# RWKV scan on one Trainium2 core: its base solved for pairs of chunks, its second half prepared inside it, and modulation weights moved to VectorE beside the feed-forward

## The chip, the cores and the metric

The kernel runs on one core of one Trainium2 chip. The metric is device microseconds of one execution. Five engines work side by side, each through a queue of its own in order: TensorE (PE in the rows; PEld is its weight load), VectorE (DVE), ScalarE (ACT), GpSimd (POOL) and SyncE (SP), which issues most DMAs.

## The reference

Two models in a row, each of several layers at width 1024. The change lies in the first one, in layer 0. It works on 256 context tokens and 256 latent tokens; its mixer is RWKV on one half of the channels (8 heads of 64, forwards and backwards) and a Mamba block on the other, then comes a gated feed-forward. What the change touches:

```
m_lat = split(silu(c)     @ w_ada[i] + b_ada[i], 6)        # modulation, 6 x 1024 values for each of
m_ctx = split(silu(c_ctx) @ w_ada[i] + b_ada[i], 6)        # 2 layers and 2 conditions
...
logw  = rw_w0 + einsum('btdl,dlc->btdc', tanh(lw), rw_w_up)
decay = exp(-exp(-softplus(-logw) - 0.5))
iclr  = sigmoid(rw_a0 + einsum('btdl,dlc->btdc', la, rw_a_up))
kk    = k * rw_k_k / max(norm(k * rw_k_k), 1e-12)
k_dir = k * (1 + (iclr - 1) * rw_k_a)
def step(S, inp):                                          # one token, both directions, context then latent
    r_t, w_t, k_t, v_t, a_t, b_t = inp                     # a = -kk, b = kk * iclr
    sa = einsum('bhvk,bhk->bhv', S, a_t)
    S  = S * w_t + sa[..., None] * b_t + v_t[..., None] * k_t
    return S, einsum('bhvk,bhk->bhv', S, r_t)
...
h = h + m[2] * mixer(modulate(rms_norm(h), m[0], m[1]))
h = h + m[5] * ((silu(x @ w1) * (x @ w3)) @ w2)            # x = modulate(rms_norm(h), m[3], m[4])
```

## The kernel before

Activations lie with channels on partitions, 128 to a tile, and 512 tokens (T, two halves of S = 256) along the free axis. Weights come from DRAM as pieces `raw` through a ring of four buffers on SyncE's queue; ScalarE rounds a piece to `whi`, VectorE takes the rest `wlo` (`split`, L347 and L348), and TensorE multiplies high and low parts in three passes (L361, L362, L364).

**The modulation.** A chunk is 256 of the 6 x 1024 outputs of one layer: 1 MB of weights. `ada_steps` runs eight matmuls a chunk, in records of 128x256 (L396), ScalarE copies the sums (`adar`, L399), two small matmuls turn and fold them (L402) and VectorE adds the bias (`mod`, L405). `ada_rest` makes a generator of such chunks that other code advances. Of the 48 chunks 26 are made during the scan (layer 0, numbers 8 to 23, and layer 1, numbers 0 to 9), and 14 in the feed-forward of layer 0, one for each of its first slots.

**The preparation.** `rwkv_prep` makes, for all 512 tokens, the cumulated decay `cs`, the products `b` and the keys `kd` of both directions, four blocks of channels one after the other. It is done before the scan starts.

**The scan.** `rwkv` cuts each direction into 8 chunks of 64 tokens; step n takes chunk n of the forward direction and the matching one of the backward direction, 16 heads in all on two sets of partitions. For a step:

- `products`: exponentials `ew`, `ei` on ScalarE, the scaled tiles `ar` and `bkp` on VectorE and GpSimd (L734 to L741), the chunk's own products masked into `g` (L750, L751), and transposes `bt`.
- `base`: the 16x16 diagonal blocks of a triangular matrix are cut out of `g` (copies L768, then L770 and L771) and inverted by 15 rounds on VectorE: a shuffle gives a row of the block to all partitions of its group (`lb`, L777), a multiply (`lm`, L780) and an add into `s` (L782). The rounds shrink from 15 columns a head to 1.
- `inverse`: the blocks are set on a diagonal (`st`, L788) and joined to 64x64 by two levels of small matmuls (L793 to L805).
- `values` and `through`: the chunk's values `uv`, its outputs, and the update of the state `X` (add L848, decay by `wc` L849).

Base and products of a step are written ahead of the step that uses them: base two steps, products three. A scheduler lays the instructions of each engine in an order of its own; the loop only gives it their sequence. `fill` advances the modulation generator at places in `rwkv`; `bonus` (L898 to L904) and `rwkv_out` (L916 to L935) follow when their half of the tokens is done, and `mix_out` is the output projection behind it. The feed-forward (`gated`, `gate0`) then has slots of 48 matmuls of the first matrix, with `silu` and the product `gs`, `ghi`, `glo` behind each (L1178 to L1181), and slots of 32 matmuls of the second, with two adds into `x` behind each (L1226).

## Time and profile before

| | us |
|---|---|
| median of 3 runs (3050.88 to 3053.53) | 3051.7 |
| profiled execution | 3049.11 |
| its span | 3047.3 |
| TensorE busy | 2935.5 (96%) |
| VectorE busy | 2113.2 (69%) |
| ScalarE busy | 1592.5 (52%) |
| GpSimd busy | 774.2 (25%) |
| mean granted TensorE clock | 0.979 of full |

Busy is the time in which an engine has at least one instruction at work; the span runs from the first instruction to the last. A share is an average over stages with different limits, so stretches are read by themselves. In the rows `<-` stands between an output and its inputs; buffer numbers are left out. A group's mean mixes shapes where it says "+14 forms". A window's row begins with its bounds and its length, and ends with GB/s of all DMAs. In a time line the first number is the start, the second the duration; consecutive instructions of one kind are put together as x2, x3.

### The profile page before, as it was taken

Reading aid. Unit: us, or ns where it says so; the run is one execution under the profiler, and the core shown is the slowest. Engines: PE = TensorE matmul, PEld = TensorE weight load, DVE = VectorE, ACT = ScalarE, POOL = GpSimd, SP = SyncE. Lnnn points to the kernel's source line nnn. Section 1 sums busy time; section 2 is a strip of 40 time slices with the busy share of each in tenths; the row PEclk is TensorE's granted clock in tenths of the full one; section 3 lists DMA queues with packets and bytes.
Section 4 is the critical chain, followed back from the end, with each engine's and each line's share of the span. In section 5 each row is a group of like instructions: output and inputs, shape, how many; then the busy total and the mean of one; then the engine's idle time right before and its main releaser. Section 6 shows DMA issues by size and latency. Waiting matters only on the chain. (4 is left out here: it accounts for less than half of the span.)

```text
span 3047.3 us, 44960 instructions
## 1 busy us (share of the span) xinstructions
PE 2935.5 (96%) x17880; PEld 2453.4 (81%) x17880; DVE 2113.2 (69%) x2953; ACT 1592.5 (52%) x2007; POOL 774.2 (25%) x719
## 2 busy tenths in 40 slices
PE   7997899999999998999999999999999999999998
PEld 5884677887888777888888888878888888888887
DVE  5658987622223654998888898977697666669665
ACT  5644223432222555777777776755445545545553
POOL 0335442211022112000000000035264534434552
PEclk9998799999999999999999999999999999999999
DMA  6222234244423334999999999955533555553453
GB/s 229 70 66 70 84 111 148 104 166 146 137 75 114 110 97 154 346 359 331 363 345 337 357 350 362 340 176 186 197 132 120 192 175 199 170 195 107 150 176 128
DMA packets 132456, 584.75 MB, mean 192 GB/s; under 512 B 11792, under 2 KB 48912, under 8 KB 79760
## 3 DMA queue, kind: packets, MB, share of 16 engines
q1 hardware_dynamic: 126592, 575.35, 53.2%
q10 hardware_dynamic: 5648, 6.47, 0.9%
q8 instruction: 142, 2.33, 0.3%
q14 instruction: 74, 0.61, 0.1%
HBM read 580.73 MB, written 1.05 MB: 191 GB/s over the span
## 5 line engine op out<-in xcount | busy, mean ns | idle before, releaser
L348 DVE TENSOR_TENSOR wlo<-raw,whi 128x2048 fp32r<-128x2048 f32 (+2 forms) x497 | 1059.3, 2139 | 243.3 <-ACT whi L347 204.9
L347 ACT ACTIVATE whi<-raw 128x2048 fp32r<-128x2048 f32 (+2 forms) x500 | 886.5, 1784 | 418.8 <-PE bank L362 195.6
L372 PE MATMUL bank<-a,whi 128*128 128x512 f32 x1408 | 355.4, 395 | 5.1 <-DVE a L1693 5.1
L372 PEld LDWEIGHTS bank<-a,whi 128*128 128x128 f32 x1408 | 256.0, 190 | 51.7 <-DVE a L1693 5.4
L1361 PE MATMUL bank<-whi,xghi 128*128 128x512 f32 x704 | 282.3, 401 | 0.0
L1362 PE MATMUL bank<-whi,xglo 128*128 128x512 f32 x704 | 276.6, 393 | 0.0
L348 POOL TENSOR_TENSOR wlo<-raw,whi 128x2048 fp32r<-128x2048 f32 x3 | 13.9, 4646 | 790.2 <-ACT whi L347 790.2
L361 PE MATMUL bank<-cathi,whi 128*128 128x512 f32 (+1 forms) x608 | 212.6, 368 | 1.4 <-ACT x L1264 1.0
L362 PE MATMUL bank<-catlo,whi 128*128 128x512 f32 (+1 forms) x608 | 211.6, 364 | 1.5 <-DVE catlo L454 1.5
L375 PEld LDWEIGHTS bank<-a,wlo 128*128 128x128 f32 x1408 | 191.8, 190 | 13.6 <-DVE wlo L348 0.4
L375 PE MATMUL bank<-a,wlo 128*128 128x256 f32 x1408 | 196.5, 283 | 0.0
L1364 PE MATMUL bank<-wlo,xghi 128*128 128x512 f32 x704 | 192.2, 394 | 0.0
L1748 POOL TENSOR_TENSOR g<-gs,g 128x256 fp32r<-128x256 f32 x88 | 153.0, 1740 | 97.3 <-ACT g L1747 97.3
L372 PE MATMUL bank<-g,whi 128*128 128x512 f32 x704 | 171.2, 391 | 0.1
L1362 PEld LDWEIGHTS bank<-whi,xglo 128*128 128x128 f32 x704 | 132.4, 188 | 26.7
L1361 PEld LDWEIGHTS bank<-whi,xghi 128*128 128x128 f32 x704 | 132.2, 188 | 27.0
L1364 PEld LDWEIGHTS bank<-wlo,xghi 128*128 128x128 f32 x704 | 129.9, 188 | 29.6 <-DVE wlo L348 2.1
L372 PEld LDWEIGHTS bank<-g,whi 128*128 128x128 f32 x704 | 128.4, 188 | 24.4 <-POOL g L1748 0.3
L1613 PE MATMUL bank<-whi,gthi 128*128 128x512 f32 x352 | 139.7, 397 | 0.0
L361 PEld LDWEIGHTS bank<-cathi,whi 128*128 128x128 f32 x608 | 114.7, 190 | 29.3 <-issue 8.3
L1613 PE MATMUL bank<-whi,gtlo 128*128 128x512 f32 x352 | 138.1, 392 | 0.0
L364 PE MATMUL bank<-cathi,wlo 128*128 128x512 f32 (+1 forms) x608 | 136.4, 362 | 0.0
(530 smaller groups left out, 5883.1 us busy)
## 6 DMA issues: line engine op xcount, KB each, us to landing
raw<-in_moei_dram SPq DMA_DIRECT2D x155, 1024.0 KB, 5.7
raw<-in_sfi_dram SPq DMA_DIRECT2D x88, 1024.0 KB, 4.8
raw<-in_moeo_dram SPq DMA_DIRECT2D x77, 1024.0 KB, 5.2
raw<-in_sfo_dram SPq DMA_DIRECT2D x64, 704.0 KB, 4.1
raw<-in_ada_dram SPq DMA_DIRECT2D x104, 256.0 KB, 3.6
raw<-in_smi_dram SPq DMA_DIRECT2D x24, 1024.0 KB, 4.8
raw<-in_ffi_dram SPq DMA_DIRECT2D x22, 1024.0 KB, 4.9
x<-in_moei_dram SPq DMA_DIRECT2D x21, 1024.0 KB, 5.8
```

What stands on the lines that cost most here:

```text
L347: self.nc.scalar.activation(like(hi, w)[:, c], w[:, c], AF.Copy)
L348: (eng or self.nc.vector).tensor_sub(like(lo, w)[:, c], w[:, c], like(hi, w)[:, c].bitcast(F32))
L361: mm(ps, l, a[0][:, ak[j]], start=start and j == 0, stop=False, skip_group_check=True)
L362: mm(ps, l, a[1][:, ak[j]], start=False, stop=False, skip_group_check=True)
L364: mm(ps, w[1][:, wk[j], f0:f0 + fn], a[0][:, ak[j]], start=False, stop=stop and j == n - 1, skip_group_check=True)
L372: mm(ps.rearrange("p i s -> p (i s)"), w[0][:, wk[j], f0:f0 + P], a[:, ak[j]].rearrange("p i s -> p (i s)"), start=start and j == 0, stop= ...
L375: mm(ps[:, 0], w[1][:, wk[j], f0:f0 + P], a[:, ak[j], 0], start=False, stop=stop and j == n - 1, skip_group_check=True)
L1361: mm(ps, a[0][:, at + k, rows], w[0][:, k, cols], start=start and n == 0, stop=False, skip_group_check=True)
L1362: mm(ps, a[1][:, at + k, rows], w[0][:, k, cols], start=False, stop=False, skip_group_check=True)
L1364: mm(ps, a[0][:, at + k, rows], w[1][:, k, cols], start=False, stop=stop and n == len(ks) - 1, skip_group_check=True)
L1613: mm(y[f], g.bitcast(F32) if self.whole else g, w[q][:, i, 512 * f:512 * f + 512], start=n == q == i == p == 0, stop=n == 10 and i == 1 an ...
L1748: nc.gpsimd.tensor_sub(lo, s, hi.bitcast(F32))
```

## The change

The preparation is made for one half of the tokens at a time. The first half stands ahead of the scan, the second behind step 0, in tiles `cs`, `b`, `kd` of 256 tokens with one buffer each. The small matrices of the decay and of `iclr` are laid in four groups of 32 rows.

The base takes one or two chunks: 16 heads in one op of 128x16x(15−k). ScalarE makes its cuts, sixteen scaled copies of 32x128 a pair, and GpSimd adds them. `lb` has one buffer and takes the product too. Products 0 to 3 and the first base precede step 0, the bases (2,3), (4,5), (6,7) come behind steps 0, 2 and 3. `ar`, `g` and `bt` get four buffers in place of three. The block-mask product moves from VectorE to GpSimd, the decay of X is one op, and the values are transposed by four 128x128 transposes instead of 64x128 halves.

Of the modulation 12 chunks stay in the scan. The other 14 join the 14 of the feed-forward, and all 28 are computed there by `ada_beside`: VectorE scales the eight 128x256 pieces of a chunk by a value per partition and adds them up in `adav`, for two conditions, and TensorE sums over the partitions by four matmuls with a column of ones.

```diff
-FILL = 6
+FILL = 2
...
+    def ada_beside(self, chunks, pool):
+        nc = self.nc
+        for i, n in chunks:
+            w = self.fetch(self.ins[f"ada{i}"][n])
+            acc = pool.tile([P, 2, 256], F32, name="adav")
+            for k in range(KB):
+                wk = w[:, 256 * k:256 * k + 256]
+                for who in range(2):
+                    c = self.cz[:, k, who:who + 1]
+                    if k == 0:
+                        nc.vector.tensor_scalar(acc[:, who], wk, c, None, op0=ALU.mult)
+                    else:
+                        nc.vector.scalar_tensor_tensor(acc[:, who], wk, c, acc[:, who], op0=ALU.mult, op1=ALU.add)
+            tr = self.bank(3, [P, 2, 2])
+            for h in range(2):
+                for who in range(2):
+                    nc.tensor.matmul(tr[:, h, who:who + 1], acc[:, who, h * P:h * P + P], self.ones[:, 0:1],
+                                     start=True, stop=True, skip_group_check=True)
...
-        def base(n):
-            c32 = pool.tile([P, 8, 32], F32, name="c32", bufs=1)
-            for q in range(4):
-                rq = slice(32 * q, 32 * q + 32)
-                at = 64 * (q // 2) + 32 * (q % 2)
-                nc.vector.tensor_copy(c32[rq], G[n][q // 2][rq, :, at:at + 32])
-            c16 = pool.tile([P, 8, 16], F32, name="c16", bufs=1)
-            nc.vector.tensor_scalar(c16, c32[:, :, 0:16], self.c("half")[:, 0:1], None, op0=ALU.mult)
-            nc.vector.scalar_tensor_tensor(c16, c32[:, :, 16:32], self.c("half")[:, 1:2], c16,
-                                           op0=ALU.mult, op1=ALU.add)
+        def base(ns):
+            m = 8 * len(ns)
+            cut = [pool.tile([P, 16, 16], F32, name=name, bufs=1) for name in ("c16", "lb")]
+            for i, n in enumerate(ns):
+                for q in range(4):
+                    rq = slice(32 * q, 32 * q + 32)
+                    at = 64 * (q // 2) + 32 * (q % 2)
+                    for k in range(2):
+                        nc.scalar.activation(cut[k][rq, 8 * i:8 * i + 8], G[n][q // 2][rq, :, at + 16 * k:at + 16 * k + 16],
+                                             AF.Copy, scale=self.c("half")[rq, k:k + 1])
+            c16 = cut[0][:, :m]
+            nc.gpsimd.tensor_add(c16, c16, cut[1][:, :m])
...
             for k in range(15):
-                lb = pool.tile([P, 8, 16], F32, name="lb", bufs=3)
-                nc.vector.stream_shuffle(lb[:, :, k + 1:], c16[:, :, k + 1:],
+                lb = pool.tile([P, 16, 16], F32, name="lb", bufs=1)
+                nc.vector.stream_shuffle(lb[:, :m, k + 1:], c16[:, :, k + 1:],
                                          [16 * (q // 16) + k for q in range(32)])
-                m = pool.tile([P, 8, 16], F32, name="lm", bufs=2)
-                nc.vector.tensor_mul(m[:, :, k + 1:], lb[:, :, k + 1:],
-                                     s[:, :, k:k + 1].to_broadcast([P, 8, 15 - k]))
-                nc.vector.tensor_add(s[:, :, k + 1:], s[:, :, k + 1:], m[:, :, k + 1:])
+                nc.vector.tensor_mul(lb[:, :m, k + 1:], lb[:, :m, k + 1:],
+                                     s[:, :m, k:k + 1].to_broadcast([P, m, 15 - k]))
+                nc.vector.tensor_add(s[:, :m, k + 1:], s[:, :m, k + 1:], lb[:, :m, k + 1:])
...
-            nc.vector.tensor_mul(st.rearrange("p h (g c) -> p h g c", g=4),
+            nc.gpsimd.tensor_mul(st.rearrange("p h (g c) -> p h g c", g=4),
...
-                        nc.vector.tensor_mul(xn[r, :, r], xn[r, :, r], wc[r].to_broadcast([64, 4, 64]))
+                    nc.vector.tensor_mul(xn, xn, wc.to_broadcast([P, 4, P]))
...
-        products(0)
-        base(0)
+        for _ in prep(0):
+            pass
+        for n in range(2):
+            products(n)
+        base((0, 1))
         values(0)
         inverse(0)
-        products(1)
-        base(1)
-        products(2)
+        for n in range(2, 4):
+            products(n)
         for n in range(8):
             through(n)
             if n < 7:
                 values(n + 1)
                 inverse(n + 1)
-            if n < 6:
-                base(n + 2)
-            if n < 5:
-                products(n + 3)
-            if n in (3, 5):
-                self.bonus(n // 4, zrw, arr)
+            if n == 0:
+                base((2, 3))
+                self.bonus(0, zrw, arr)
+                for _ in prep(1):
+                    pass
+            if n == 1:
+                products(4)
+                products(5)
+            if n == 2:
+                base((4, 5))
+                products(6)
+            if n == 3:
+                products(7)
+                base((6, 7))
+                self.bonus(1, zrw, arr)
...
-                    self.rwkv(zrw, arr, lg, cat[:, 0:4], rw, self.ada_rest([(0, n) for n in range(8, 24)] + [(1, n) for n in range(EARLY)], rw, 0, 1))
+                    self.rwkv(zrw, lg, cat[:, 0:4], rw, self.ada_rest([(0, n) for n in range(8, 20)], rw, 0, 1))
...
-            beside = self.ada_rest([(1, n) for n in range(EARLY, 24)], w, 3)
+            beside = self.ada_beside([(0, n) for n in range(20, 24)] + [(1, n) for n in range(24)], w)
```

How the instructions move on VectorE at the beginning of a base. Before, the cuts of a chunk (`c`) stand between the masks of its products, three shuffles run ahead, and an op covers 8 heads:

```order
L768 COPY c_3277<-g_2910 32x256 x2
L770 TENSOR_SCALAR c_3282<-c_3277,cst_scan 128x128
L771 SCALAR_TENSOR_TENSOR c_3282<-c_3277,cst_scan,c_3282 128x128
L805 TENSOR_TENSOR st<-st,bank_2784 128x512
L777 STREAM_SHUFFLE lb<-c_3282 128x8x15
L777 STREAM_SHUFFLE lb<-c_3282 128x8x14
L777 STREAM_SHUFFLE lb<-c_3282 128x8x13
```

Now, in the base of chunks 2 and 3 (L821, L823 and L825 are the shuffle, the multiply and the add):

```order
L823 TENSOR_TENSOR lb<-lb,s_2785 128x16x15
L825 TENSOR_TENSOR s_2785<-s_2785,lb 128x16x15
L821 STREAM_SHUFFLE lb<-c_2766 128x16x14
L823 TENSOR_TENSOR lb<-lb,s_2785 128x16x14
L825 TENSOR_TENSOR s_2785<-s_2785,lb 128x16x14
L821 STREAM_SHUFFLE lb<-c_2766 128x16x13
L850 TENSOR_TENSOR st<-st,bank_2391 128x512
```

The cuts have left the queue, an op covers 16 heads, and the shuffle of a turn stands behind the add of the turn before.

VectorE in the feed-forward, before, in a slot of the first matrix and, from `x` on, of the second:

```order
L1179 TENSOR_TENSOR gs<-gs,bank_6885 128x512
L348 TENSOR_TENSOR wlo<-raw,whi 128x2048
L405 TENSOR_TENSOR mod_68<-bank_6940,par 128x4
...
L1226 SCALAR_TENSOR_TENSOR x<-bank_7118,mod_67,x 128x256 x2
L348 TENSOR_TENSOR wlo<-raw,whi 128x1408
L405 TENSOR_TENSOR mod_68<-bank_7155,par 128x4
```

and now (L344 is the split, L1233 the product `gs`, L1280 the add into `x`, L422, L424 and L431 the new chain and its bias):

```order
L422 TENSOR_SCALAR adav<-raw,c_59 128x256 x2
L424 SCALAR_TENSOR_TENSOR adav<-raw,c_59,adav 128x256 x14
L1233 TENSOR_TENSOR gs<-gs,bank_6180 128x512
L344 TENSOR_TENSOR wlo<-raw,whi 128x2048
L431 TENSOR_TENSOR mod_68<-bank_6253,par 128x4
...
L422 TENSOR_SCALAR adav<-raw,c_59 128x256 x2
L424 SCALAR_TENSOR_TENSOR adav<-raw,c_59,adav 128x256 x11
L1280 SCALAR_TENSOR_TENSOR x<-bank_6944,mod_67,x 128x256 x2
L344 TENSOR_TENSOR wlo<-raw,whi 128x1408
```

The sixteen ops of a chunk stand in the queue ahead of the `gs` and `wlo` of their slot.

## Rows read from the trace of the kernel before

**Rows 1.** Windows: busy us (records) of PE, PEld, DVE, ACT, POOL; clock, DMA share.

```profile
235.00:548.00 313.00, 269.56 (x3165) 204.97 (x3165) 262.10 (x821) 103.90 (x198) 129.18 (x159) 0.91 0.30 100
270.00:346.00 76.00, 59.66 (x605) 44.52 (x605) 64.68 (x252) 17.86 (x41) 43.31 (x61) 0.74 0.41 136
600.00:1000.00 400.00, 400.00 (x2148) 327.77 (x2147) 126.32 (x152) 110.47 (x127) 70.02 (x30) 1.00 0.37 127
```

**Rows 2.** Time line of VectorE: first add into X of steps 0, 5, 6.

```profile
346.29 0.86 DVE L848 TENSOR_TENSOR X<-X,bank 64x256 f32<-64x256 f32 x2
...
513.96 0.86 DVE L848 TENSOR_TENSOR X<-X,bank 64x256 f32<-64x256 f32 x2
...
529.46 0.87 DVE L848 TENSOR_TENSOR X<-X,bank 64x256 f32<-64x256 f32 x2 [0.34 <-PE bank L843]
```

**Rows 3.** VectorE's groups, 235 to 548 us; after the bar busy us, mean ns.

```profile
L780 DVE TENSOR_TENSOR lm<-lb,s 128x120 f32<-128x120 f32 (+14 forms) x120 | 39.7, 332 | 0.5
L782 DVE TENSOR_TENSOR s<-s,lm 128x120 f32<-128x120 f32 (+14 forms) x120 | 37.3, 311 | 3.1
L777 DVE STREAM_SHUFFLE lb<-c 128x120 f32<-128x120 f32 (+14 forms) x120 | 26.9, 234 | 0.0
...
L849 DVE TENSOR_TENSOR X<-X,wc 64x256 f32<-64x256 f32 x28 | 15.0, 536 | 0.6
L768 DVE COPY c<-g 32x256 f32<-32x256 f32 x32 | 14.2, 445 | 0.6
...
L788 DVE TENSOR_TENSOR st<-s,cst_scan 128x512 f32<-128x512 f32 x8 | 6.0, 754 | 0.2
...
L771 DVE SCALAR_TENSOR_TENSOR c<-c,cst_scan,c 128x128 f32<-128x128 f32 x8 | 4.9, 617 | 0.1
L899 DVE SCALAR_TENSOR_TENSOR b<-kd,par,b 128x256 f32<-128x256 f32 x8 | 4.8, 628 | 0.0
L405 DVE TENSOR_TENSOR mod<-bank,par 128x4 f32<-128x4 f32 x26 | 4.0, 153 | 4.9 <-PE bank L402 4.6
```

**Rows 4.** Time line of VectorE in the normalisation ahead of the feed-forward.

```profile
593.91 1.27 DVE L447 SCALAR_TENSOR_TENSOR nx<-x,gs,nrs 128x256 f32<-128x256 f32 x3
...
596.61 0.48 DVE L447 SCALAR_TENSOR_TENSOR nx<-x,gs,nrs 128x256 f32<-128x256 f32 x1
```

**Rows 5.** Time line of VectorE in the base.

```profile
293.64 0.27 DVE L780 TENSOR_TENSOR lm<-lb,s 128x120 f32<-128x120 f32 x1
...
314.18 0.69 DVE L780 TENSOR_TENSOR lm<-lb,s 128x16 f32<-128x16 f32 x1
...
337.46 1.21 DVE L782 TENSOR_TENSOR s<-s,lm 128x96 f32<-128x96 f32 x1
...
345.20 0.17 DVE L780 TENSOR_TENSOR lm<-lb,s 128x8 f32<-128x8 f32 x1
```

**Rows 6.** GpSimd's groups, 235 to 548 us.

```profile
L691 POOL TENSOR_TENSOR b<-zrw,ic 128x512 f32<-128x512 f32 x8 | 15.8, 2014 | 29.8 <-DVE zrw L689 27.3 <-ACT ew L732 2.5
L740 POOL TENSOR_TENSOR bkp<-kd,ei 64x256 f32<-64x256 f32 x16 | 13.1, 825 | 13.8 <-PE bank L758 9.6 <-ACT adar L399 3.8
```

**Rows 7.** ScalarE's groups, 235 to 548 us: one table load.

```profile
L732 ACT ACT_TABLE_LOAD x1 | 1.3, 1283 | 0.0
```

**Rows 8.** TensorE's groups, 235 to 548 us, the modulation.

```profile
L396 PE MATMUL bank<-raw,c 128*32 128x256 f32 x416 | 42.7, 452 | 19.4 <-DVE mod L405 13.4 <-ACT pq L677 3.9 <-DMA raw<-in_ada_dram 1.2
L402 PE MATMUL bank<-cst_all,adar 128*128 128x2 f32 x104 | 16.5, 263 | 4.0 <-ACT adar L399 4.0
```

**Rows 9.** Time line of TensorE: the modulation in one slot of the feed-forward.

```profile
649.86 1.07 PE L396 MATMUL bank<-raw,c 128*32 128x256 f32 x16
...
656.11 0.50 PE L402 MATMUL bank<-cst_all,adar 128*128 128x2 f32 x4
```

**Rows 10.** Windows of a slot of the first matrix and one of the second.

```profile
649.86:662.73 12.87, 12.87 (x69) 9.82 (x69) 3.05 (x3) 3.46 (x5) 2.61 (x1) 1.00 0.47 164
785.16:792.63 7.47, 7.47 (x34) 6.20 (x33) 2.40 (x3) 1.38 (x1) 0.00 (x0) 1.00 0.42 140
```

More of the change, by code (lines that the diff above doesn't have):

```diff
@@ L168, in host_arrays @@
     A["par"] = pk.array()
-    lo = _Pack()
-    for d in range(2):
-        lo.add(f"w_up{d}", _rows_to(g["rw_w_up"][0, d], at=32 * d))
-        lo.add(f"a_up{d}", _rows_to(g["rw_a_up"][0, d], at=64 + 32 * d))
-    lo.add("g_up", _rows_to(g["rw_g_up"][0]))
-    A["lora"] = lo.array()
+    A["lora"] = np.concatenate([
+        np.concatenate([g["rw_w_up"][0].reshape(64, 512), g["rw_a_up"][0].reshape(64, 512)], axis=0),
+        _rows_to(g["rw_g_up"][0])], axis=1)
     A["router"] = np.ascontiguousarray(
@@ L189, in host_arrays @@
         A[f"cst_{name}"] = pack.array()
-    return A, pk.at, lo.at, {name: pack.at for name, pack in cst.items()}
+    return A, pk.at, {name: pack.at for name, pack in cst.items()}
 def _consts():
@@ L660, in rwkv_prep @@
         nc.vector.tensor_scalar(ka1, self.p("k_a"), -1.0, 1.0, op0=ALU.mult, op1=ALU.add)
-        nc.sync.dma_start(lg[:, 0], self.ins["lora"][:, 2048:2560])
-        ssp = self.bank(2, [8, T])
+        nc.sync.dma_start(lg[:, 0], self.ins["lora"][:, 512:1024])
+        return lora, reset, tl, ka1
+    def rwkv_prep(self, half, zrw, arr, made, pool):
+        nc = self.nc
+        mm = nc.tensor.matmul
+        lora, reset, tl, ka1 = made
+        at = slice(S * half, S * half + S)
+        ssp = self.bank(2, [8, S])
         for j in range(4):
-            kq = pool.tile([P, T], F32, name="pq")
-            nc.scalar.activation(kq, zrw[:, j], AF.Square, scale=self.p("k_k", j))
+            kq = pool.tile([P, S], F32, name="pq")
+            nc.scalar.activation(kq, zrw[:, j, at], AF.Square, scale=self.p("k_k", j))
             mm(ssp, self.c("sel")[:, 8 * j:8 * j + 8], kq, start=j == 0, stop=j == 3)
-        nrm = pool.tile([8, T], F32, name="pq")
+        nrm = pool.tile([8, S], F32, name="nrm", bufs=1)
         nc.scalar.activation(nrm, ssp, AF.Sqrt)
@@ L670, in rwkv_prep @@
         nc.vector.reciprocal(nrm, nrm)
+        yield
         for j in range(4):
-            ic = [pool.tile([P, T], F32, name=f"ic{d}") for d in range(2)]
+            ic = [pool.tile([P, S], F32, name=f"ic{d}") for d in range(2)]
+            acc = [self.bank(k, [P, S]) for k in (1, 1, 2, 2)]
+            for q in range(4):
+                r = slice(32 * q, 32 * q + 32)
+                mm(acc[q], lora[r, j * P:(j + 1) * P], tl[r, at], start=True, stop=True)
             for d in range(2):
-                wp = self.bank(0, [P, T])
-                mm(wp, lora[:, o[f"w_up{d}"] + j * P:o[f"w_up{d}"] + (j + 1) * P], tl, start=True, stop=True)
-                sg = pool.tile([P, T], F32, name="pq")
-                nc.scalar.activation(sg, wp, AF.Sigmoid, bias=self.p(f"w0{d}", j))
+                sg = pool.tile([P, S], F32, name="pq")
+                nc.scalar.activation(sg, acc[d], AF.Sigmoid, bias=self.p(f"w0{d}", j))
                 back = slice(None, None, -1) if d else slice(None)
@@ L701, in rwkv @@
         first, second = (up, dn), (dn, up)
+        both = ((0, up), (1, dn))
         bcast = lambda m, n: m[:, None, :].to_broadcast([m.shape[0], n, m.shape[1]])
@@ L713, in rwkv, with prep @@
         S16 = {}
+        made = self.rwkv_first(lg, pool)
+        arr = {}
+        def prep(half):
+            arr.update({k: pool.tile([P, 2, 4, S], F32, name=k, bufs=1) for k in ("cs", "b", "kd")})
+            return self.rwkv_prep(half, zrw, dict(arr), made, pool)
         def tokens(n):
@@ L722, in products @@
             ch, tok = tokens(n)
+            c0, c1 = (k % 4 for k in ch)
+            own = [slice(64 * c0, 64 * c0 + 64), slice(64 * c1 + 63, 64 * c1 - 1 if c1 else None, -1)]
             ew = pool.tile([P, 2, 4, 65], F32, name="ew", bufs=1)
@@ L810, in values @@
             vp = self.bank(0, [P, 4, P], 0)
-            vr = pool.tile([P, 4, 64], F32, name="vr", bufs=1)
-            nc.gpsimd.tensor_copy(vr, zrw[:, 8:12, tok[1]])
+            vr = pool.tile([P, 4, P], F32, name="hh", bufs=1)
             for d, rows in ((1, up), (0, dn)):
-                for j in range(4):
-                    mm(vp[rows, j], vr[:, j] if d else zrw[:, 8 + j, tok[0]], ident, start=True, stop=True,
-                       skip_group_check=True)
+                nc.gpsimd.tensor_copy(vr[:, :, rows], zrw[:, 8:12, tok[d]])
+            for j in range(4):
+                tr(vp[:, j], vr[:, j], ident)
+            for d, rows in ((1, up), (0, dn)):
                 ev(uv[rows, d], vp[rows].rearrange("p j (h v) -> p (j h) v", h=2))
@@ L896, in bonus @@
         for j in range(4):
[L897 to L899 removed]
+            e = arr["b"][:, 1, j]
+            nc.vector.tensor_scalar(e, arr["kd"][:, 0, j], self.p("r_k0", j), None, op0=ALU.mult)
+            nc.vector.scalar_tensor_tensor(e, arr["kd"][:, 1, j], self.p("r_k1", j), e,
                                            op0=ALU.mult, op1=ALU.add)
```

71 lines of the change are left out of this document (34 added, 37 removed).

## The prediction

> **What bounds the kernel now.** The profiled execution has a span of 3047.3 us. I cut it into windows first, to see where TensorE, which works nearly all of it, has gaps. Two stretches matter here. The RWKV scan with its preparation, 235 to 548 us, is 313 us long; VectorE works 262.1 of them, TensorE 269.6, GpSimd 129, ScalarE 104. In the feed-forward behind it TensorE works all of 400 us and VectorE 126 [rows 1]. So a microsecond off VectorE can count in the scan, and one off TensorE counts in the feed-forward. Within the scan VectorE stands still for only 313 − 262 = 51 us. TensorE's busy share is as high, but there it does short matmuls that follow one another in small dependent groups; its granted clock of 0.74 in the ramp (270 to 346) means that it was at the lower of its two levels for a good part, and it works only 59.7 of those 76 us. What a step costs when little else is asked of VectorE is seen at the scan's end: the updates of X in steps 5 and 6 begin at 513.96 and 529.46, 15.5 us apart, while from step 0 (346.29) to step 5 there are 168 us, 33.5 a step [rows 2]. The 18 us between are VectorE's other work.
>
> **What VectorE does there.** The triangular base (multiply, add, shuffle, 120 of each) has 39.7 + 37.3 + 26.9 us of records, its cuts L768 and L771 14.2 + 4.9: 123.0 us [rows 3]. Records of one engine overlap: three of 0.48 us take 1.27 in a run, not 1.44 [rows 4]. With the same 12% off, the base occupies 108 us.
>
> **The base in pairs.** The 120 triples become 60 of twice the columns (mean 128 in place of 64; 4 pairs of 1920, 7680 columns in all). Undisturbed, a multiply of 120 columns takes 0.27 us and one of 8 takes 0.17 [rows 5]: about 0.165 us and 0.9 ns a column. Sixty multiplies and sixty adds: 120 × 0.165 + 2 × 7680 × 0.0009 = 33.6 us. A shuffle has a mean of 0.234 at 64 columns [rows 3], so 0.29 at 128, and sixty take 17.5. Together 51 us, with no overlap, since one buffer `lb` makes the three ops of a turn wait for one another. The groups' means (0.332 and 0.311) are above 0.22 because ops are disturbed: a multiply of 16 columns takes 0.69 us, an add of 96 takes 1.21 [rows 5], both beside GpSimd. That is 0.1 us an op; I keep 0.1, 12 us for 120 ops: 63 in all. VectorE gives up 108 − 63 = 45 us, 33 to 57 with the disturbance doubled or gone.
>
> **The scan's other edits.** X's decay as one op of 128x512 (0.75 by L788's mean, which has the same shape) for two of 0.54: 28 × 0.536 − 14 × 0.75 = 4.5 us less. The product with the block mask, 6.0 us, goes to GpSimd. Fourteen modulation adds fewer: 14 × 0.15 = 2. The preparation in halves makes twice the instructions, 28 more at 0.165 fixed: 4.6 us more. VectorE is left with 262 − 45 − 4.5 − 6 − 2 + 4.6 = 209 us. GpSimd gains eight mask products, 2.0 us each by L691's shape, 16 us, and eight copies and four adds of at most 0.8 (L740), of which I take half: 5; it comes to 150 [rows 6]. ScalarE gains 64 cuts of 32x128, which no row has (the nearest is the same cut on VectorE, L768, 0.445 for twice the columns, also the upper end; I take 0.3): 19 us. Its Sigmoid, Sqrt and Exp now alternate, eight more table loads of 1.28: 10 [rows 7]. It comes to 133. TensorE loses 14 of 26 modulation chunks at (42.7 + 16.5)/26 = 2.3 us: 32 [rows 8]. None of the three becomes fuller than VectorE.
>
> **What that is on the path.** With the same 51 us of standing still the stretch takes 209 + 51 = 260 in place of 313: −53. But work moves to engines for which VectorE then waits. Products need eight GpSimd ops of about 0.8 us a chunk, 6.6, and four chunks' products now precede the first step; scaled cuts and an add stand ahead of every base; the second half's preparation is queued behind step 0, products 4 and 5 behind it. I charge 3 us: **−50**. Laid out: first X at about 340 with four bases done, step 4 at about 435, then 15.5 a step, and the output projection at about 498. Bounds: the stalls grow to 80 us (−25), or shrink to 30 (−75).
>
> **The modulation in the feed-forward.** On TensorE 14 chunks go: L396 takes 1.07 us and L402 0.50 in a slot [rows 9]: 14 × 1.6 = −22. In come 28 × 4 matmuls of one column against a 128x128 weight, which no row has; the nearest is L402, two matmuls of two columns with such a weight, 0.50 as records and 0.4 where they overlap their neighbours. Four make 0.8: +22. Net 0 (half and double of it: −11 to +22; the row is so near that I use ±5).
>
> On VectorE a chunk brings two scaled copies and fourteen scalar-tensor-tensor of 128x256. L447, of the same form, takes 1.27 us for three in a run, 0.40 from start to start [rows 4]: sixteen take 6.3 us, 7.7 at full records of 0.48. A slot of the first matrix is 12.87 us long with 3.05 of VectorE [rows 10]; after the change about 12.0 with 9.3: hidden, cover 2.7 us. A slot of the second matrix is 7.47 us with 2.40 [rows 10]; it becomes 8.3 with 8.7. Eight such slots fall 3 us behind, which the second buffer of `adav` takes: 0, bounds −5 and +10. Each slot's chain stands ahead of `gs` and `wlo` in the queue, so past that cover it is `wlo`, and with it TensorE, that comes late.
>
> At the start of the feed-forward the first two chains, 12.5 us, are mixed into the second half of the normalisation, for which TensorE waits next: +4 (0 if its queue still holds matmuls, 8 if most of the chains fall in between). 28 MB of modulation weights instead of 14 meet a DMA share of 0.37 [rows 1]: hidden; without that cover a late piece costs a few microseconds.
>
> **Sum.** −50 + 0 + 4 = −46 on the profiled 3049.1 (span and 1.8 around it): 3003. The runs' median lies 2.6 above that execution: **3006 us**.
>
> **Rivals.** *New waits.* Products paced by GpSimd, table loads ahead of the second preparation, serial pairs: one late `c16` holds every X behind it in VectorE's queue. For it: three more steps lie between engines. Against: GpSimd and ScalarE are below half full. Stalls of 80: −25 + 4, 3031.
>
> *GpSimd's new work holds VectorE up.* The add of 1.21 us is longer than an undisturbed one by about the 0.9 to 1.3 that GpSimd's ops take. If all 21 us that GpSimd gains fall on VectorE, the scan gives −29 and the time is 3027. The Trainium skill, page "SBUF — State Buffer", section on the shared port pair, would have it so: a VectorE instruction with two SBUF inputs and a GpSimd instruction that reads SBUF exclude each other, the later waiting in full. The disturbed rows agree in size. Against the whole price: VectorE works only 209 of 260 us then, and its shuffles and ops on PSUM are not of that kind.
>
> *Stalls shrink.* With four bases ahead the 15.5 us step is reached early: −75, 2981. For it: TensorE's clock would rise in the ramp; against: products 4 to 7 and two bases still come between.
>
> *VectorE bounds the feed-forward*, and the kernel is slower. L899, of the chain's form and size, takes 0.63 us in the scan [rows 3]. At 0.65 an op, first-matrix slots ask 3.05 + 10.4 = 13.5 of 12.0 and second-matrix ones 12.8 of 8.3: 20 × 1.5 + 8 × 4.5 = 66 us, 3072. It outweighs the scan from about 0.61 us an op. Against it: GpSimd works 2.6 us a slot and none in the second kind [rows 10].
>
> *Given back in full*, at about 0.6 us an op: 3052.
>
> **Chances.** Forecast 0.47 (own range 2990 to 3020), new waits 0.16, GpSimd 0.10, shrinking stalls 0.12, feed-forward bound 0.10, given back 0.05. A measurement of this kernel tells some 0.2%, 6 us, from no change. Faster 0.84, same 0.05, slower 0.11. The range leaves out the last two cases and the outer tails of the others: 2976 to 3036.
>
> **What would show it.** VectorE busy near 210 us from 235 us to the output projection, which begins near 498; sixty multiplies and adds of the base at 0.3 to 0.4 us; first X near 340; a clock above 0.74 in the ramp. In the feed-forward the chain's ops 0.40 apart and TensorE without gaps. The prediction is wrong if VectorE stands still for over 80 us of the scan, if the chain's ops start over 0.6 apart, or if TensorE waits for `adav` or `wlo`.

## The result and the profile after

The changed kernel takes 3073.25 us (median of 4 runs, 3071.17 to 3078.91) beside 3052.55 for the kernel before: a ratio of 1.0073, 95% interval 1.006 to 1.0086. The forecast was 3006 with a range up to 3036. The kernel became 21 us slower. The profiled execution has a span of 3069.4 us, 22.1 more than before.

The windows of the changed kernel that answer to [rows 1] (columns as there):

```profile
235.00:548.00 313.00, 247.83 (x2727) 196.65 (x2728) 212.68 (x512) 131.24 (x266) 137.81 (x177) 0.79 0.15 51
270.00:346.00 76.00, 52.58 (x568) 41.93 (x564) 53.42 (x146) 27.00 (x64) 41.82 (x55) 0.77 0.25 84
548.00:561.00 13.00, 7.82 (x119) 6.41 (x116) 6.80 (x16) 6.50 (x14) 0.91 (x2) 0.89 0.08 19
600.00:1000.00 400.00, 396.48 (x2028) 335.65 (x2028) 309.19 (x612) 101.39 (x111) 70.71 (x30) 1.00 0.44 157
```

VectorE lost the work that it was to lose: 212.7 us up to 548 and 6.8 up to 561 are 219.5, beside 262.1 before and 209 forecast. But the stretch did not shrink. The output projection, which was to begin near 498, begins at 562.57 instead of 547.57 (time line of TensorE):

```profile
562.57 0.80 PE L357 MATMUL bank<-cathi,whi 128*128 128x512 f32 x1 [6.29 <-ACT whi L343]
```

So VectorE stands still for 326 − 219.5 = 106 us where it stood for 51. The granted clock of the whole stretch fell from 0.91 to 0.79. The first additions into X of steps 0 to 6 (time line of VectorE; before, [rows 2]):

```profile
351.34 0.84 DVE L893 TENSOR_TENSOR X<-X,bank 64x256 f32<-64x256 f32 x2
388.20 0.83 DVE L893 TENSOR_TENSOR X<-X,bank 64x256 f32<-64x256 f32 x2
431.73 0.84 DVE L893 TENSOR_TENSOR X<-X,bank 64x256 f32<-64x256 f32 x2
453.45 0.84 DVE L893 TENSOR_TENSOR X<-X,bank 64x256 f32<-64x256 f32 x2
499.86 0.84 DVE L893 TENSOR_TENSOR X<-X,bank 64x256 f32<-64x256 f32 x2
522.42 0.85 DVE L893 TENSOR_TENSOR X<-X,bank 64x256 f32<-64x256 f32 x2 [0.52 <-PE bank L888]
536.14 0.85 DVE L893 TENSOR_TENSOR X<-X,bank 64x256 f32<-64x256 f32 x2 [4.07 <-PE bank L888]
```

The first X comes at 351 (forecast 340), and steps 1 and 2 take 37 and 44 us, with the second preparation and products 4 and 5 beside them. Step 4 takes 46 (its X comes at 499.86, forecast 435); before, the longest, step 5, took 47. In it VectorE waits 4.6 us for GpSimd's add of the last pair's cuts and then works mainly on that pair; TensorE meanwhile joins the blocks of step 4 and waits 3.9 and 2.5 us for VectorE's share in this, which stands between the pair's ops (time lines of VectorE and TensorE):

```profile
477.93 0.01 DVE L821 LOAD_MASK_SELECT lb<-c  x1 [4.55 <-POOL c L816]
...
483.77 1.98 PE L845 MATMUL bank<-tt,lmask 64*64 64x64 f32 x32 [3.94 <-DVE tt L838]
...
493.00 1.97 PE L881 MATMUL bank<-z,st 64*64 64x64 f32 x32 [2.48 <-DVE st L850]
```

From the first X to that of step 6 both kernels take nearly the same time; windows before and after:

```profile
346.29:529.46 183.17, 168.80 (x2282) 137.75 (x2281) 154.05 (x511) 58.64 (x115) 69.22 (x87) 0.97 0.30 102
351.34:536.14 184.80, 153.33 (x1824) 128.15 (x1824) 123.73 (x283) 79.02 (x152) 84.41 (x104) 0.81 0.04 16
```

VectorE works 30 us less in these steps, and they are not shorter. Another 8 us go behind them: from the X of step 6 to the output projection the changed kernel takes 26.4 us, before 18.1. The mixer's outputs must be rounded (`cathi`) ahead of the projection. Before, ScalarE began that 24 us ahead of the projection; now it does it right ahead of the projection's weights `whi`, for which TensorE waits 6.29 us, as the row at 562.57 shows, instead of 0.40:

```profile
523.42 1.15 ACT L947 ACTIVATE cathi<-x 128x512 fp32r<-128x512 f32 x2 [3.97 <-PE bank L903]
547.57 0.60 PE L361 MATMUL bank<-cathi,whi 128*128 128x512 f32 x1 [0.40 <-ACT whi L347]
```

```profile
556.37 2.19 ACT L1005 ACTIVATE cathi<-x 128x512 fp32r<-128x512 f32 x4 [1.42 <-issue]
```

The groups of VectorE show that the ops themselves are priced right (235 to 560 us; beside [rows 3]):

```profile
L825 DVE TENSOR_TENSOR s<-s,lb 128x240 f32<-128x240 f32 (+14 forms) x60 | 25.6, 426 | 1.6
L823 DVE TENSOR_TENSOR lb<-lb,s 128x240 f32<-128x240 f32 (+14 forms) x60 | 23.1, 385 | 1.6
...
L821 DVE STREAM_SHUFFLE lb<-c 128x240 f32<-128x240 f32 (+14 forms) x60 | 19.1, 318 | 0.0
...
L894 DVE TENSOR_TENSOR X<-X,wc 128x512 f32<-128x512 f32 x14 | 10.3, 737 | 0.3
```

The base is 67.8 us of records, 63 forecast. The clock by stretch (0.50 is the lower of its two levels, 1.00 the upper) shows a new thing. Windows of the changed kernel, the first two in the first preparation, the third beside the second:

```profile
250.00:260.00 10.00, 9.11 (x55) 4.50 (x54) 8.73 (x17) 7.72 (x18) 4.26 (x5) 0.50 0.42 148
260.00:270.00 10.00, 7.49 (x38) 3.83 (x38) 4.92 (x12) 4.12 (x9) 5.01 (x8) 0.50 0.48 166
...
370.00:410.00 40.00, 34.75 (x203) 25.72 (x203) 23.53 (x40) 22.18 (x37) 15.62 (x21) 0.54 0.00 1
```

and of the kernel before, in its preparation and at the later time:

```profile
240.00:260.00 20.00, 16.47 (x34) 5.22 (x32) 18.98 (x20) 10.00 (x15) 8.03 (x4) 1.00 0.00 1
370.00:410.00 40.00, 37.20 (x510) 32.24 (x510) 38.07 (x140) 10.90 (x21) 15.69 (x20) 0.96 0.16 54
```

TensorE is busy for 91% of a stretch with the clock at the lower level, 0.50, and before it was busy for 82% of one with the clock at the upper level. The feed-forward went nearly as forecast; VectorE now works 309 of the 400 us [rows 1] and TensorE 396. A slot of each matrix, beside [rows 10]:

```profile
703.48:715.61 12.13, 12.13 (x59) 9.94 (x58) 9.99 (x19) 3.15 (x3) 2.60 (x1) 1.00 0.50 170
794.05:802.48 8.43, 8.43 (x42) 7.09 (x41) 8.15 (x19) 1.38 (x1) 0.00 (x0) 1.00 0.56 192
```

The slots are 12.13 and 8.43 us long (12.0 and 8.3 forecast), VectorE works 10.0 and 8.2 of them, and TensorE has no gap. The chain's ops take (9.99 − 3.05)/16 = 0.43 and (8.15 − 2.40)/16 = 0.36 us, not 0.61. Only the start is late: the first `gs` comes at 641.23 instead of 618.40, 22.8 us, of which the output projection had lost 15.

### The profile page after: what moved, and what is told of

Read it like the earlier page. It is cut to its first block, busy times and chain, and to the rows that moved or that the text cites. A ratio compares the mean times of both kernels' runs of the same rounds, so it can differ in the third digit from the quotient of the medians.

```text
span 3069.4 us, 44349 instructions
## 1 busy us (share of the span) xinstructions
PE 2924.1 (95%) x17496; PEld 2466.9 (80%) x17496; DVE 2258.0 (74%) x3121; ACT 1623.4 (53%) x2072; POOL 788.9 (26%) x743
## 5 line engine op out<-in xcount | busy, mean ns | idle before, releaser
L344 DVE TENSOR_TENSOR wlo<-raw,whi 128x2048 fp32r<-128x2048 f32 (+2 forms) x497 | 1060.5, 2138 | 241.9 <-ACT whi L343 206.4
L344 POOL TENSOR_TENSOR wlo<-raw,whi 128x2048 fp32r<-128x2048 f32 x3 | 13.9, 4649 | 793.0 <-ACT whi L343 793.0
L371 PEld LDWEIGHTS bank<-a,wlo 128*128 128x128 f32 x1408 | 191.7, 190 | 13.2
L424 DVE SCALAR_TENSOR_TENSOR adav<-raw,c,adav 128x256 f32<-128x256 f32 x392 | 163.8, 483 | 0.0
```

What stands on the lines that cost most here:

```text
L344: (eng or self.nc.vector).tensor_sub(like(lo, w)[:, c], w[:, c], like(hi, w)[:, c].bitcast(F32))
L371: mm(ps[:, 0], w[1][:, wk[j], f0:f0 + P], a[:, ak[j], 0], start=False, stop=stop and j == n - 1, skip_group_check=True)
L424: nc.vector.scalar_tensor_tensor(acc[:, who], wk, c, acc[:, who], op0=ALU.mult, op1=ALU.add)
```

## The experiments

Fourteen kernels, each with the kernel before on the same chip. "Old modulation" means 26 chunks in the scan and 14 in the feed-forward, all on TensorE, as before.

**The modulation apart from the scan.** First question: did the scan lose because fourteen chunks that had filled TensorE's gaps were gone?

New scan, old modulation:

```diff
-FILL = 2
+FILL = 6
-... self.ada_rest([(0, n) for n in range(8, 20)], rw, 0, 1)
+... self.ada_rest([(0, n) for n in range(8, 24)] + [(1, n) for n in range(10)], rw, 0, 1)
-beside = self.ada_beside([(0, n) for n in range(20, 24)] + [(1, n) for n in range(24)], w)
+beside = self.ada_rest([(1, n) for n in range(10, 24)], w, 3)
```

> The changed scan with all 26 modulation chunks back on TensorE in it (six offered a step) and 14 in the feed-forward on TensorE, as before the change. Theory A (the filler): the changed scan lost time because fourteen chunks that filled TensorE's gaps were gone, its granted clock fell to the lower level (0.50 in 320-350, 373-411 and 480-497 us) and every dependent matmul group took longer; then the clock stays above 0.85 from 270 to 500 us, the output projection begins near 510 and the time is 3000 to 3030. Theory B (the new order): the waits of the serial pairs, of the second preparation beside the scan and of GpSimd's product cost it whatever fills TensorE; then the scan stays as long as in the changed kernel or longer, and only the feed-forward's start gets its 8 us back: 3060 to 3075.

3081.3 us, ratio 1.0102 (1.0086 to 1.0119). Old scan, new modulation (the same edits the other way round, in the kernel before):

> The scan of before, with twelve chunks in it, two offered a step, and 28 chunks on VectorE in the feed-forward. Theory A: the old scan too loses clock where the chunks filled TensorE (below 0.85 from 270 to 500 us) and grows by 10 to 30 us; with +8 for the feed-forward's start and -2 for its slots the time is 3068 to 3090. Theory B: the old scan, bound by VectorE, is as long as before or some microseconds shorter: 3050 to 3060.

3049.7 us, ratio 0.9997 (0.9987 to 1.0007). And the changed kernel with matmuls that nobody needs:

```diff
+def idle(n):
+    acc = self.bank(0, [P, 256], 1)
+    for k in range(KB):
+        g = k % 4
+        mm(acc[32 * g:32 * g + 32], self.cz[:, k], AR[n][:, 0, 0:2], start=k < 4, stop=k >= 4, ...)
...
+            if n < 5:
+                for _ in range(3):
+                    idle(n + 1 if n < 3 else n)
```

> The changed kernel with fifteen groups of eight matmuls (128x32 by 256 columns, the shape of a modulation chunk) on data of the scan, three behind each of the steps 0 to 4, whose sums nobody reads: TensorE gets work in its gaps, and no other engine and no DMA gets any. Theory A: the clock rises above 0.80 in 373-411 and 480-497 us and the time falls by 15 to 45 us: 3028 to 3058. Theory B: the added matmuls only lengthen TensorE's queue: 3073 to 3095.

3082.8 us, ratio 1.0105 (1.0089 to 1.0122). Windows 235 to 548 of the three, in this order:

```profile
235.00:548.00 313.00, 272.12 (x2865) 202.52 (x2865) 203.40 (x511) 131.91 (x271) 136.41 (x175) 0.81 0.29 94
```

```profile
235.00:548.00 313.00, 263.22 (x2917) 206.29 (x2916) 272.23 (x814) 104.28 (x188) 132.38 (x159) 0.85 0.17 57
```

```profile
235.00:548.00 313.00, 261.90 (x2808) 194.33 (x2808) 202.36 (x495) 129.32 (x259) 135.31 (x175) 0.80 0.14 47
```

Theory A falls. The new scan is 31 us slower with all its chunks back, at a clock of 0.81. Moving the chunks costs the old scan nothing in sum: its output projection begins 8.5 us earlier (539.03), its first `gs` only 0.9 us earlier (617.54). Useless matmuls cost some 10 us. They hardly change the clock of the whole stretch (0.79 without them, 0.80 with them), but in the three stretches that the first expectation names it is 0.68, 0.63 and 0.80 instead of 0.50, 0.51 and 0.50: a higher clock that comes with useless work gave no time back. Most of the loss is in the new scan, whatever fills TensorE.

**The parts of the new scan, each alone in the kernel before.** Pairs (the base of the change with its cuts, three buffers):

```diff
-        base(0)
...
+        products(1)
+        base((0, 1))
...
-            if n < 6:
-                base(n + 2)
             if n < 5:
                 products(n + 3)
+            if n in (0, 2, 4):
+                base((n + 2, n + 3))
```

> The kernel of before with the base for pairs of chunks and its cuts on ScalarE and GpSimd, and nothing else: three buffers, whole preparation ahead of the scan, modulation as before; the pairs come behind steps 0, 2 and 4, the first ahead of step 0. Both theories expect VectorE busy 35 to 50 us less in the scan. Theory O (VectorE's occupancy bounds the scan, and what cost the changed kernel its gain lies elsewhere): 3005 to 3030. Theory P (a pair is one long serial block in VectorE's queue, in front of which TensorE empties and behind which X and the products wait, so that the saved time returns as gaps): 3045 to 3075.

3061.5 us, ratio 1.0035 (1.002 to 1.0049). Halves (the change's preparation, with the functions `base`, `inverse`, `values`, `through` and the order of before):

```diff
+            if n == 0:
+                self.bonus(0, zrw, arr)
+                for _ in prep(1):
+                    pass
+            if n == 5:
+                self.bonus(1, zrw, arr)
```

> The kernel of before with the preparation in halves, the second behind step 0, and nothing else: base of single chunks on VectorE, old order of products and bases, three buffers, old inverse, values, decay and modulation. Theory H (the second preparation beside the scan is what costs: its ops wait for ScalarE's table loads and for TensorE, and steps 1 and 2 wait behind them): 3065 to 3085, the scan's first X earlier than 346 by about 10 us and that of step 2 later than 402. Theory P (the pairs cost, the halves do not): 3040 to 3055.

3071.6 us, ratio 1.0062 (1.0045 to 1.0079). Relief in place (the cuts of single chunks on ScalarE and GpSimd, X's decay as one op, order of before):

```diff
-                nc.vector.tensor_copy(c32[rq], G[n][q // 2][rq, :, at:at + 32])
+                for k in range(2):
+                    nc.scalar.activation(cut[k][rq], G[n][q // 2][rq, :, at + 16 * k:at + 16 * k + 16],
+                                         AF.Copy, scale=self.c("half")[rq, k:k + 1])
...
+            nc.gpsimd.tensor_add(c16, c16, cut[1])
```

> The kernel of before with two reliefs of VectorE and no other order: the cuts of a base as eight scaled copies on ScalarE and an add on GpSimd (19 to 22 us off VectorE) and the decay of X as one op (4.5 us). If VectorE's occupancy bounds the scan of before, as the prediction's first step had it, the time falls by most of that: 3027 to 3040. If the chain between the engines bounds it and VectorE's occupancy is only high, the cuts' way over two engines costs what VectorE saves: 3045 to 3060.

3044.8 us, ratio 0.9981 (0.9972 to 0.9991). Windows of the three:

```profile
235.00:548.00 313.00, 271.37 (x3054) 200.27 (x3054) 215.57 (x522) 120.46 (x252) 131.27 (x155) 0.88 0.30 100
```

```profile
235.00:548.00 313.00, 271.77 (x3089) 210.25 (x3090) 255.31 (x829) 111.34 (x211) 121.61 (x159) 0.83 0.28 91
240.00:270.00 30.00, 24.43 (x148) 12.79 (x144) 17.89 (x36) 18.07 (x34) 10.00 (x14) 0.67 0.47 160
```

```profile
235.00:548.00 313.00, 276.08 (x3187) 208.16 (x3187) 247.73 (x761) 129.63 (x263) 133.52 (x167) 0.92 0.31 104
```

These windows have fixed ends, and a scan that ends sooner has later work in them. Up to the start of each kernel's own output projection (before, relief in place, pairs):

```profile
235.00:547.57 312.57, 269.13 (x3163) 204.64 (x3162) 261.67 (x821) 103.47 (x198) 129.18 (x159) 0.91 0.30 101
235.00:540.96 305.96, 269.04 (x3162) 202.44 (x3161) 240.69 (x758) 125.56 (x261) 133.52 (x167) 0.92 0.31 103
235.00:557.97 322.97, 279.20 (x3164) 206.69 (x3163) 220.16 (x533) 126.40 (x262) 133.08 (x159) 0.88 0.30 97
```

The relief takes 21 us of VectorE's work out of the stretch without any new order, and 6.6 come back: VectorE stands still for 65 us in place of 51. So VectorE's work is worth about a third of itself here. Pairs cost 10 us although VectorE works 42 less. Halves cost 20, with 5 us more of VectorE's work. The two prices add up to about the 31 of the whole new scan, which has further edits; that they simply add is not shown.

**Why the halves cost.** The four small matrices had been padded to 128 rows; the change stacks them and its matmuls use 32 rows each. Halves alone with the padding back:

```diff
-                r = slice(32 * q, 32 * q + 32)
-                mm(acc[q], lora[r, j * P:(j + 1) * P], tl[r, at], start=True, stop=True)
+                o = 512 * (0, 2, 1, 3)[q] + j * P
+                mm(acc[q], lora[:, o:o + P], tl[:, at], start=True, stop=True)
```

> Halves alone (3071.6), but with the small matrices of the preparation padded to 128 rows as before the change, so that its matmuls use all rows of TensorE. In the halves kernel TensorE's clock fell to 0.50 at 260-270 and 0.67 at 380-400 us although it was busy 77 to 91% there, with matmuls of 32 rows. Theory K (narrow matmuls let the clock fall, and the steps beside them run at the lower level): the clock stays above 0.85 at 375-400 and the time is 3050 to 3062. Theory Q (the second preparation, with its table loads, stands in the queues of TensorE and ScalarE in front of step 1): unchanged, 3066 to 3080.

3056.2 us, ratio 1.0015 (1.0006 to 1.0025). And both halves ahead of the scan, with 32 rows:

```diff
-                    self.rwkv_prep(zrw, lg, arr, pool(c, "pw", 2))
+                    pw = pool(c, "pw", 2)
+                    made = self.rwkv_first(lg, pw)
+                    for half in range(2):
+                        for _ in self.rwkv_prep(half, zrw, {k: t[:, :, :, S * half:S * half + S] for k, t in arr.items()}, made, pw):
+                            pass
```

> The kernel of before with the preparation in two halves and with small matrices of 32 rows, but both halves ahead of the scan; nothing else. Theory Q: the halves cost only their instructions, 3050 to 3058. Theory K: the narrow matmuls cost clock here too and the ramp grows by 8 to 20 us: 3059 to 3072.

3068.1 us, ratio 1.0063 (1.0044 to 1.0081). Windows in the preparation and beside the second one, 128 rows, then of the second kernel, 32 rows:

```profile
240.00:270.00 30.00, 25.48 (x134) 13.91 (x134) 13.85 (x30) 15.74 (x32) 6.99 (x11) 0.89 0.55 185
375.00:400.00 25.00, 23.82 (x250) 17.61 (x249) 24.50 (x57) 14.30 (x27) 15.03 (x21) 1.00 0.26 85
```

```profile
240.00:270.00 30.00, 25.61 (x64) 13.59 (x65) 21.55 (x41) 17.25 (x33) 6.62 (x8) 0.52 0.06 20
```

TensorE is equally busy, 25.5 and 25.6 of 30 us, and the clock is 0.89 with 128 rows and 0.52 with 32. These two stretches differ in more than the rows, since 9.3 us of the first are modulation matmuls and the second has none. Halves alone, which differs from the first kernel in the rows only, had 24.4 us and 0.67 there. The second kernel has a closer partner in the kernel before, whose window of 240 to 260 us stands above (16.47 us busy at 1.00):

```profile
240.00:260.00 20.00, 16.43 (x41) 8.84 (x42) 15.33 (x29) 10.24 (x21) 6.02 (x8) 0.52 0.08 29
```

The padding gives 14 of the 20 us back, and putting the halves ahead gives next to nothing: its first X comes at 360.24, 14 us later than before. So most of it is the narrow matmuls and hardly the place of the second preparation or its table loads. The 6 us that are left with 128 rows are about as long as TensorE's wait ahead of the output projection. In the eight kernels here that prepare the second half inside the scan, the changed one among them, that wait is 5.7 to 6.3 us, and in the other eight, the kernel before among them, 0.2 to 1.6. The change also moved `cs`, `b` and `kd` into the scan's own buffers; whether the roundings come late for that was not tried.

The groups of these matmuls, 235 to 420 us, halves alone first, then with 128 rows:

```profile
L706 PE MATMUL bank<-sqsum,lora 32*128 32x256 f32 x64 | 16.1, 472 | 1.1 <-ACT ic L713 0.8 <-ACT pq L709 0.3
```

```profile
L709 PE MATMUL bank<-sqsum,lora 128*128 128x256 f32 x64 | 20.2, 432 | 0.0
```

With 32 rows they take 16.1 us of TensorE and with 128 rows 20.2. The Trainium skill, page "TensorE: Matmul & The Clock Gate", Part 3 on packing small matmuls, lets four matmuls of 32 rows in different row groups run side by side, 3.07 times as fast as one after the other (measured there with 512 columns). By that rule the stacked form wins; here a fifth is saved, and the kernel is 14 us slower. Where four do follow one another, they overlap: in the first row below eight records take 0.71 us. Later in the same half they come in runs of one to six records (halves alone, time line of TensorE):

```profile
242.69 0.71 PE L706 MATMUL bank<-sqsum,lora 32*128 32x256 f32 x8
...
255.55 1.22 PE L706 MATMUL bank<-sqsum,lora 32*128 32x256 f32 x2
```

That the padding gives time back was shown by putting it back; that it does so through the clock, which rises with it, is argued only.

**Why the pairs cost.** Two buffers for the shuffled rows, in the pairs-alone kernel:

```diff
-lb = pool.tile([P, 16, 16], F32, name="lb", bufs=1)
+lb = pool.tile([P, 16, 16], F32, name="lb", bufs=2)
```

> Pairs alone (3061.5), but with two buffers for the shuffled rows, so that a shuffle can run ahead of the multiply and add of its turn. If the strict turn of shuffle, multiply and add is what costs: 3045 to 3054. If the pair's length as one block between the steps, and the two chunks of products that it waits for, are what cost: 3056 to 3066.

3054.5 us, ratio 1.0007 (0.9998 to 1.0017): the strict turn of three ops is most of the 10 us. The rest is not told from nothing here. But both kernels with pairs have the relief's cuts in them; beside the relief in place (3044.8), which also has the one-op decay, pairs with two buffers are still some 8 to 10 us slower.

**The single gains together.** Relief in place with the new modulation:

> The scan of before with the cuts on ScalarE and GpSimd and the one-op decay (alone 6.6 us faster), and the modulation as after the change (alone no change): 14 chunks less for TensorE in the scan as well as 24 us less for VectorE. If either engine's relief is hidden behind the other's work, both together give more than their sum: 3028 to 3040. If a chain of waits through all engines sets the scan's time: the sum, 3042 to 3048.

3037.7 us, ratio 0.9957 (0.994 to 0.9974), the fastest of all. Relief alone gives 6.6, the move alone nothing, both 12.6. Up to the output projection they give 6.6, 8.5 and, together, 20.2 us (it begins at 527.39), of which the start of the feed-forward takes some 8 back. That is one execution each, but it is what one sees where neither VectorE nor TensorE bounds the scan alone.

**The same causes in the changed kernel.** To have room for padded matrices two raw buffers (of four) and one buffer of `ic` (of two) go; first that control, then the padding on top:

```diff
-RAWS = 4
+RAWS = 2
-            ic = [pool.tile([P, S], F32, name=f"ic{d}") for d in range(2)]
+            ic = [pool.tile([P, S], F32, name=f"ic{d}", bufs=1) for d in range(2)]
```

> The changed kernel (3073) with two raw buffers instead of four in the scan and one buffer for the two sigmoids of the preparation, which makes room; a control for the next run. Theory: the modulation pieces and the sigmoids wait a little more, 3070 to 3085.

> The control kernel just before with the small matrices of the preparation padded to 128 rows, and nothing else. If matmuls of 32 rows cost the changed kernel its clock (halves alone: 20 us with 32 rows, 6 with 128), the clock at 250-270 and beside the second preparation rises above 0.80 and the time is 10 to 18 us below the control. If that held only with the modulation's matmuls beside them, which the changed kernel has moved away: within 5 us of the control.

The control takes 3085.6 us, ratio 1.0107 (1.009 to 1.0124); with 128 rows 3066.4, ratio 1.0047 (1.003 to 1.0063). Control first:

```profile
240.00:270.00 30.00, 23.82 (x88) 10.77 (x88) 12.33 (x25) 20.43 (x34) 4.80 (x9) 0.50 0.23 81
370.00:410.00 40.00, 34.69 (x324) 25.26 (x323) 21.70 (x39) 20.65 (x36) 10.63 (x13) 0.83 0.04 15
```

```profile
240.00:270.00 30.00, 25.27 (x108) 13.09 (x110) 14.31 (x30) 16.25 (x33) 6.72 (x10) 0.73 0.36 125
370.00:410.00 40.00, 32.56 (x394) 23.95 (x396) 26.44 (x47) 24.87 (x43) 17.97 (x23) 0.99 0.00 1
```

Padding alone is worth 19 us in this kernel, nearly as much as the change lost, but the control with its smaller buffers is itself some 10 us slower than the changed kernel. Then all of the change with padding, two shuffle buffers and the order and three buffers of the pairs-alone kernel:

> All parts of the change, with 128 rows in the preparation, two buffers for the shuffled rows, and the order of the pairs-alone kernel (three buffers; pairs behind steps 0, 2 and 4, products three steps ahead). By the sum of the single effects: 3073 - 14 - 7 = 3052, and 3040 to 3056 with the order unknown. If the four products and two bases ahead of step 0 were what helped the changed kernel: 3058 or more.

3063.9 us, ratio 1.0043 (1.0028 to 1.0057): 9 better than the change, but 8 above the upper end of what the single effects promised with the order unknown. Last, the fastest version with pairs and two buffers:

> The fastest version so far (cuts on ScalarE and GpSimd, one-op decay, new modulation: 3037.7) with the base in pairs and two buffers for the shuffled rows. If VectorE's work still sets that scan, the pairs' 20 us and more show as 5 to 15 us: 3023 to 3033. If a pair's block between the steps costs what it saves, as with the old modulation: 3034 to 3044.

3052.5 us, ratio 1.0004 (0.9994 to 1.0013): the pairs take the whole 13 us away again. Windows of this kernel and of the fastest version at the same place, in which the former solves the pair (2, 3):

```profile
370.00:410.00 40.00, 29.53 (x416) 27.11 (x415) 27.15 (x78) 12.46 (x26) 14.33 (x18) 0.79 0.01 1
```

```profile
370.00:410.00 40.00, 34.00 (x470) 30.32 (x469) 35.81 (x116) 13.95 (x32) 16.26 (x21) 0.96 0.01 2
```

With the pair every engine works less in the same 40 us and TensorE's clock falls. That is what a serial block between the steps looks like; which instruction waits first was not isolated.

**Where each kernel loses it.** Starts in us, from one profiled execution each, as read from the time lines of VectorE (X, `gs`) and TensorE (output projection):

| | first X | X of step 6 | output projection | first `gs` |
|---|---|---|---|---|
| before | 346.29 | 529.46 | 547.57 | 618.40 |
| changed | 351.34 | 536.14 | 562.57 | 641.23 |
| old scan, new modulation | 348.81 | 518.87 | 539.03 | 617.54 |
| halves alone | 343.34 | 542.90 | 569.82 | 639.90 |
| halves alone, 128 rows | 345.05 | 531.80 | 555.96 | 625.36 |
| all of the change, repaired | 338.57 | 527.06 | 552.22 | 631.12 |

The changed kernel loses 5.0 us up to the first X, 1.6 in the steps, 8.3 from there to the output projection and 7.8 up to the first `gs`: 22.8. The padding of the halves gives its time back between the first X and step 6. The repaired kernel is 8.2 us behind the old scan with the same modulation at step 6 and 13.2 at the output projection.

## Why the prediction was wrong

The step that failed is "with the same 51 us of standing still the stretch takes 209 + 51 = 260": the work on VectorE was forecast within 11 us and the stalls doubled, from 51 to 106. The forecast charged 3 us for all new waits. I read an engine that works 84% of a stretch as its bound. The relief in place shows what it is: 21 us less of VectorE's work up to the output projection, 6.6 us less time, and the stalls grow from 51 to 65 with no new order at all. The work goes from engine to engine, and each one's idle time depends on the order.

*The base in pairs*: forecast 63 us, measured 67.8; the saving on VectorE is right. All new waits together were priced at 3 us; the pairs alone cost 10 in the kernel before. The sentence that one buffer makes the three ops of a turn wait for one another took from it only that VectorE's records do not overlap: most of the 10 us are this buffer.

*The preparation in halves*: I counted 4.6 us of fixed cost and table loads. It costs 20, of which 14 go with the padding to 128 rows; the late rounding ahead of the output projection, some 6 us, had no term either. I had read the four groups of 32 rows in the diff and given them no price, neither as a term nor as a rival. The clock was in my list only as something that would rise in the ramp; it fell in the scan as a whole, from 0.91 to 0.79.

*The modulation moved*: net about nothing, but this is partly luck. The old scan with the new modulation is within 0.1%, since 8.5 us that the forecast did not count come back in the scan and 7.7 are lost at the start of the feed-forward. TensorE's slots are within 0.13 us of the forecast, the chain's ops at 0.36 to 0.43 us, and in the changed kernel the start of the feed-forward lost 22.8 − 15.0 = 8 us, the upper bound of that term. The rival that ended slower, VectorE bounding the feed-forward, did not happen: that its 3072 is near the time measured is chance.

*New waits* was the rival with the right kind of cause and the wrong size: its stalls of 80 us gave −25, the 106 measured gave +15 at the output projection. The late `c16` that it names is seen: VectorE waits for that add twice, 9.5 us in all, 4.6 of them in step 4. *GpSimd's new work*: the ops of the base hold 0.1 to 0.15 us of disturbance each, about as priced, and VectorE waits 2.4 us in all for the block-mask product (`tt` behind `st`, 235 to 560 us), so that product is not seen as a main cause; it was not put back alone.

Open: how the loss divides among its causes. The pairs and the narrow matmuls each cost something in kernels of their own, and the late rounding is read from the traces; their prices were not taken out of the changed kernel one by one. Padding is worth 19 us in a kernel with fewer buffers, so whether the changed kernel with its own buffers and 128 rows would equal the kernel before was not tried, for room. In the repaired kernel 13 us remain. By the table, against the old scan with the same modulation, 8 of them are there at step 6, which would fit the pairs, and 5 come from there to the output projection, where this kernel too has the late rounding. The order was not varied further.

## What to carry to other kernels

An engine that works five sixths of a stretch of short dependent work need not be its bound: take a little work off it in place, without a new order, and see what comes back before reordering for it. Merging small ops into long serial ones saved the engine here and cost its neighbours; a second buffer gave most of the price of pairs alone back, but not the gain, so look at where the other engines stand during the block. Packing small matrices to use fewer rows of TensorE saves memory, but here the padded zeros were worth 14 to 19 us, and the clock was higher with them (0.89 against 0.67, 0.73 against 0.50). Look also at what stands in the queues where one stage ends and the next begins: 6 us were lost there without any instruction becoming longer.

## What the runs showed of the hardware

With nothing but the rows of the preparation's matmuls changed, from 32 to 128, mostly zeros, the granted clock from 240 to 270 us rose from 0.67 to 0.89 in one pair of kernels, with TensorE busy for 24.4 and 25.5 us, and from 0.50 to 0.73 in another, with 23.8 and 25.3. In two kernels in which TensorE has only the preparation from 240 to 260 us (before, and halves ahead) it was busy for 16.4 and 16.5 of 20 us; the clock was 0.52 with 32 rows and 1.00 with 128, whose matmuls also have twice the columns. In the changed kernel the clock was 0.50, the lower level, for 20 us in which TensorE was busy for 83%, the preparation's matmuls of 32 rows among them; in the kernel before it was 1.00, the upper level, at 82% with 128 rows. I had taken a low clock as a sign of gaps only. With added matmuls in the shape of the modulation, with a weight of 32 columns, the clock of 235 to 548 us was 0.80, without them 0.79.
